# One F32 product per norm row, twelve warm-up matmuls and squares behind later casts in a decoder-trunk kernel

## The chip, the cores and the metric

The kernel runs on one NeuronCore of a Trainium2 chip. The time is device time in microseconds of one execution, from start to end; lower is better. An execution's span, from its first to its last instruction, is a little shorter than its time.

Five engines work side by side, each through its own instructions in order: PE (TensorE, matrix products), ACT (ScalarE), DVE (VectorE), POOL (GpSimd) and SP (SyncE, which here only starts transfers). They wait for each other through semaphores. PE's products go to PSUM, which ACT and DVE read; the other tiles stand in SBUF.

## The reference

One layer of a decoder trunk on 256 prompt tokens and 8 x 4 sample tokens, 2048 channels, all in F32:

```python
def trunk_layer(x, ...):
    h = rmsnorm(x, norm1_g)
    proj = einsum("btd,de->bte", h, w_in) + b_in           # 2048 -> 3072
    a, gate, z = proj[..., :1024], proj[..., 1024:2048], proj[..., 2048:]
    u = a * sigmoid(gate)
    u_ext = concatenate([hist_conv, u], axis=1)
    c = silu(layernorm(depthwise_causal_conv(u_ext, conv_w, conv_b), ln_g, ln_b))   # 31 taps
    z_ext = concatenate([hist_pool, z], axis=1)
    d = multiscale_pool(z_ext, pos0)                        # windows of 2, 4, 8, 16
    p = einsum("btgc,gce->btge", d, pool_w).reshape(bsz, T, 1024) * pool_scale
    x = x + einsum("btm,md->btd", concatenate([c, p], -1), w_out)
    h2 = rmsnorm(x, norm2_g)
    f = square(relu(einsum("btd,df->btf", h2, w_ff1)))      # 2048 -> 8192
    x = x + einsum("btf,fd->btd", f, w_ff2)
    return x, u_ext[:, -30:], z_ext[:, -15:]

def rmsnorm(x, g):
    return x * rsqrt(mean(x * x, axis=-1) + 1e-6) * g
```

A last rmsnorm follows. The layernorm over the 1024 conv channels subtracts the mean and divides by the root of the variance. So there are four places where a mean over channels becomes one inverse root per token.

## The kernel before, in words

**Layout.** Channels stand on the 128 partitions, the 288 tokens (T) along the row: `xT` has 16 slices (k) of 128 x 288. A weight matrix times activations is a run of 128 x 128 weight tiles, each with 288 columns streaming through.

**Precision.** A weight block `wr` comes by transfer from memory in F32. ACT casts it to `whi`, in a one-pass format (fp32r), and the rest `wlo` = `wr` - `whi` is formed on DVE (L279, in the first blocks L372), on POOL (L282, in two halves) or by a second transfer that accumulates (L277). Activations are split in the same way. Each weight tile then takes three matmuls: high by high, `wlo` by high, `whi` by low. `split_part` (L268) does this; which engine takes a block is set by the table `WAYS`.

**PE's order** is the program's order: `chain` (L300 to L308) ties each matmul behind the one before. `gemm` (L310) writes the products of a block, two weight slices (a pair of k) at a time; `between={key: f}` calls `f`, which puts a small product of its own into the row of matmuls at that place, and `classes` permutes the first few matmuls of a block. On the other engines a scheduler orders the instructions by a time model at build, with `later()` marking the conv taps as work for gaps.

**Start.** Nine F32 matmuls on a tile of ones (`warm`, L214) run while the first transfers are under way. `first_split` (L358) then takes the pairs of slices of `xT` as they land: it casts the weights of the first two conv heads (`whi`, L363, L370; `wlo`, L372) and scales x by the gain into `hx` (L366, L368, L375). The first `gemm` (L532) makes two conv heads, 192 matmuls; it isn't normalised yet. `squares` (L410) sums x squared over the slices: ACT squares a pair of slices (L417), DVE adds (L419 to L421), in the buffer `z_all`, into `tot`.

**First norm.** `rsqrt_sums` (L238), called by `first_sums` in the last pair of that gemm, brings the sums over the partitions onto 96 partitions x 3 columns (three small products, `pt`), and computes the inverse root there with a Sqrt on ACT and one Newton step on DVE (`st`, L249 to L256). `spread` (L259), called by `first_rows` behind the twelfth matmul of the third conv head, brings it back to a row on every partition by three products with the identity; `rb` (L529) is the row. The conv heads' results are multiplied by it afterwards (L444).

**Middle.** `SEQUENCE` (L45) gives the order of conv heads (c), pool projections (p) and pool products (P). `conv_pair` (L439) puts a head through gate, 31 taps on DVE (L460) and a reduction (L465); `pool_group` (L476) does window sums on POOL (L491 to L499) and splits the result to `dx` (L501, L502); `pool_products` (L507) multiplies it by pool_w. `sum_c` on POOL adds the conv outputs. Then the output projection runs in eight groups (L593), the pool half first; the layernorm is computed meanwhile through the table `BETWEEN` (L591): in group 5 `ln_mean` (L568), two F32 products over `sum_c` and the last conv output; in group 6 `ln_sums` (L573), the variance by `rsqrt_sums`; in group 7 `ln_rows`, `spread`. The normalised, gated result `mx` feeds the conv half of the projection.

**Second norm.** `second_rows` (L656), in the second group of the MLP: one matrix `means` on PE, Sqrt on ACT, and `inverse_root` (L231: a reciprocal and three more DVE instructions on 128 x 288).

**End.** The MLP takes four chunks of 2048 hidden channels; x is stored after the last norm, whose 96 x 3 inverse root (L726, L727) stands between the last products and the stores.

## Time and profile before

| | |
|---|---|
| median of 3 runs | 1083.33 us (1083.02 to 1084.15) |
| profiled execution: time, span | 1083.32 us, 1081.2 us |
| mean granted TensorE clock over the span | 0.997 |
| busy: PE, DVE, ACT, POOL | 99%, 59%, 44%, 16% |
| matmul records on PE | 8198 |
| read from memory | 185.16 MB, mean 175 GB/s over the span with what is written |

The busy times count instructions that overlap in the pipeline, so a busy PE says only that it never stood empty for long. What the kernel loses on PE is seen in the spacing of its matmuls: where PE is fed, one 128 x 288 matmul of the one-pass format starts every 0.13 us (572.63 us for the 4404 of the longest unbroken run). A row of the timeline gives the start, the length up to the last end, the engine, line and operation, the tiles and the count; in brackets stands the idle time ahead of it and what ended it. An F32 product leaves two records, so nine warm-up matmuls are 18.

### The profile page before, as it was taken

The page shows a single profiled execution, that of the slowest core. Times are in us where ns is not written, and L with a number is a line of the kernel's source. Part 1 is how long each engine was busy: PE and PEld are TensorE (multiplying, and loading weights), DVE is VectorE, ACT ScalarE, POOL GpSimd, SP SyncE. Part 2 cuts the span into 40 slices and gives each one's busy share as a digit, 9 for nine tenths or more (in the row PEclk, how much of TensorE's full clock was granted, in tenths as well). Part 3 has the DMA queues.
Part 4 walks back from the last instruction along what each step waited for, and adds up shares of the span by engine and source line. Part 5 has one row for each costly group of instructions (what it writes and reads, how often), then busy time and mean ns, then how long its engine had stood idle before and what let it go on. Part 6 is the DMA issues. An engine that isn't in the chain of part 4 may idle for free.

```text
span 1081.2 us, 19573 instructions
## 1 busy us (share of the span) xinstructions
PE 1069.8 (99%) x8198; PEld 1068.7 (99%) x8198; DVE 636.8 (59%) x818; ACT 477.6 (44%) x585; POOL 174.6 (16%) x180
## 2 busy tenths in 40 slices
PE   9999999999999999999999999999999999999996
PEld 9999999999999999999999999999999999999996
DVE  7899999787754544444554444555544445554553
ACT  8654445565544433334443333444433334444441
POOL 0878979512000000000000000000000000000001
PEclk9999999999999999999999999999999999999998
DMA  9896468555555555555555555555555555555522
GB/s 327 281 272 184 140 187 250 172 170 170 166 173 164 171 173 165 170 171 164 172 173 162 172 168 168 171 173 163 173 170 165 172 173 163 172 170 165 172 79 88
DMA packets 58296, 190.71 MB, mean 176 GB/s; under 512 B 6240, under 2 KB 11232, under 8 KB 58208
## 3 DMA queue, kind: packets, MB, share of 16 engines
q1 hardware_dynamic: 56336, 184.35, 54.5%
q0 software_dynamic: 1008, 3.67, 1.9%
q8 instruction: 64, 1.05, 0.4%
q10 hardware_dynamic: 864, 1.44, 0.4%
q14 instruction: 24, 0.20, 0.1%
HBM read 185.16 MB, written 4.28 MB: 175 GB/s over the span
## 4 chain that ended last, share of the span: by engine, by line
PE 76%; issue 20%; DMA 2%; DVE 1%; ACT 0%; POOL 0%; SPq 0%; POOLq 0%; DVEq 0%
PE ac L305 75%; DMA wr<-in_w 1%; PE pp L305 1%; DMA u_all<-in_hist_c 0%; DVE wlo L279 0%; POOL xT L738 0%; PE pt L305 0%; ACT whi L363 0%; DVE hx L375 0%; DVE st L255 0%; DVE wlo L372 0%; PE pmean L305 0%; ACT hx L368 0%; SPq L191 0%; POOLq L788 0%
## 5 line engine op out<-in xcount | busy, mean ns | idle before, releaser
L274 ACT CAST whi<-wr 128x1024 fp32r<-128x1024 f32 (+1 forms) x332 | 346.5, 1044 | 553.6 <-PE ac L305 540.6
L279 DVE TENSOR_TENSOR wlo<-wr,whi 128x1024 fp32r<-128x1024 f32 x288 | 353.6, 1228 | 346.0 <-ACT whi L274 346.0
L305 PE MATMUL ac<-ax,whi 128*128 128x288 f32 x2048 | 351.0, 292 | 0.0
L305 PE MATMUL ac<-fx,whi 128*128 128x288 f32 x2048 | 350.2, 292 | 0.0
L305 PEld LDWEIGHTS ac<-ax,whi 128*128 128x128 f32 x2048 | 296.0, 187 | 0.0
L305 PEld LDWEIGHTS ac<-fx,whi 128*128 128x128 f32 x2048 | 295.6, 187 | 0.0
L305 PE MATMUL ac<-ax,wlo 128*128 128x288 f32 x1024 | 217.3, 292 | 0.0
L305 PE MATMUL ac<-fx,wlo 128*128 128x288 f32 x1024 | 216.4, 292 | 0.0
L305 PEld LDWEIGHTS ac<-ax,wlo 128*128 128x128 f32 x1024 | 162.6, 187 | 0.0
L305 PEld LDWEIGHTS ac<-fx,wlo 128*128 128x128 f32 x1024 | 162.2, 187 | 0.0
L305 PE MATMUL ac<-hx,whi 128*128 128x288 f32 x768 | 131.1, 294 | 1.4 <-DVE hx L366 1.4
L738 POOL TENSOR_TENSOR xT<-xT,rf 128x288 f32<-128x288 f32 x4 | 3.1, 796 | 800.1 <-ACT rf L742 800.1
L305 PEld LDWEIGHTS ac<-hx,whi 128*128 128x128 f32 x768 | 111.8, 189 | 1.6 <-ACT hx L368 1.6
L282 POOL TENSOR_TENSOR wlo<-wr,whi 128x512 fp32r<-128x512 f32 x74 | 101.5, 1420 | 35.7 <-ACT whi L274 34.6
L460 DVE SCALAR_TENSOR_TENSOR pc<-u_all,vec,pc 128x256 f32<-128x256 f32 x232 | 99.4, 481 | 1.9 <-ACT pc L457 0.7
L305 PE MATMUL ac<-hx,wlo 128*128 128x288 f32 x384 | 80.1, 294 | 0.0
L305 PEld LDWEIGHTS ac<-hx,wlo 128*128 128x128 f32 x384 | 60.9, 189 | 0.1
L305 PE MATMUL ac<-dx,whi 128*128 128x288 f32 x256 | 46.9, 294 | 0.0
L305 PE MATMUL ac<-mx,whi 128*128 128x288 f32 x256 | 44.6, 292 | 0.0
L682 DVE SCALAR_TENSOR_TENSOR t<-ac,r 128x576 f32<-128x576 f32 x32 | 24.2, 758 | 25.3 <-PE ac L305 25.3
L305 PEld LDWEIGHTS ac<-dx,whi 128*128 128x128 f32 x256 | 38.4, 188 | 0.1
L305 PEld LDWEIGHTS ac<-mx,whi 128*128 128x128 f32 x256 | 37.4, 187 | 0.0
(133 smaller groups left out, 535.2 us busy)
## 6 DMA issues: line engine op xcount, KB each, us to landing
wr<-in_w SPq DMA_DIRECT2D x335, 512.0 KB, 3.8
wlo<-in_w POOLq DMA_DIRECT2D x7, 512.0 KB, 8.2
xT<-in_xT SPq DMA_DIRECT2D x8, 288.0 KB, 7.7
wr<-in_w SPq DMA_DIRECT2D x5, 256.0 KB, 3.7
out_u_out<-u_all SPq DMA_DIRECT2D x1, 1208.0 KB, 9.1
u_all<-in_hist_c SPq DMA_DIRECT2D x8, 136.0 KB, 5.2
out_z_out<-z_all SPq DMA_DIRECT2D x1, 668.0 KB, 9.9
z_all<-in_hist_p SPq DMA_DIRECT2D x4, 152.0 KB, 6.9
```

The lines of the kernel that those rows point to most:

```text
L274: nc.scalar.copy(hi, raw)
L279: nc.vector.tensor_tensor(lo, raw, f32(hi), op=ALU.subtract)
L282: nc.gpsimd.tensor_tensor(lo[:, j : j + 2, :], raw[:, j : j + 2, :], f32(hi[:, j : j + 2, :]), op=ALU.subtract)
L305: last = nc.tensor.matmul(*args, **kw)
L460: nc.vector.scalar_tensor_tensor(out=dst, in0=up[:, w : w + SEQ], scalar=cwv[:, w : w + 1], in1=pc, op0=ALU.mult, op1=ALU.add)
L682: nc.vector.scalar_tensor_tensor(out=t, in0=bk[:, :, :T], scalar=0.0, in1=both(rows2[0]), op0=ALU.max, op1=ALU.mult)
L738: eng.tensor_tensor(xk, xk, r[:, None, :].to_broadcast([P, n, T]), op=ALU.mult)
```

## The change

1. Warm-up: twelve `warm` matmuls for nine.
2. Norm rows: `rsqrt_sums`, `spread` and `inverse_root` go. `row_of_sums` makes one F32 product of the 128 x 128 constant `minus` (-0.5 / 2048 everywhere) with the 128 x 288 sums, which gives -0.5 times the mean on every partition at once. `row_of` takes the inverse root of the row by ACT's Abs_reciprocal_sqrt, its square by ACT, and one Newton step in two DVE instructions. The first row (`first_row`) stands whole behind the twelfth matmul of the third conv head; the product with `ones` in the last pair of the first gemm is gone. The layernorm's product stands where `ln_sums` stood; `ln_rows` is gone. The layernorm row comes out halved, so `ln_g` is doubled once on POOL.
3. The layernorm's mean: one product for two. ACT copies `sum_c` to PSUM, DVE adds the last conv output to it.
4. Second and last norm: the same inverse root, without the reciprocal. The last one has four short instructions for five.
5. Squares of x: the square of pair q is issued behind the scaling of a later slice (`scaled`): pairs 0 to 3 behind the `hx` of the fifth pair, each later one behind that of the pair after it, which leaves the last two behind the last pair.
6. The first twelve matmuls of the third conv head stand in their natural order, for the permuted one.

```diff
-        return nc.scalar.activation(few[: src.shape[0], :], src, func)
-    load_table(AF.Sqrt, ones[:, 0:1])
+        return nc.scalar.activation(few[: src.shape[0], :], src, func, scale=0.0, bias=1.0)
+    load_table(AF.Abs_reciprocal_sqrt, ones[:, 0:1])
     warm = ms("warm")
-    for j in range(9):
+    for j in range(12):
         nc.tensor.matmul(warm[:, 0, 0:P], ones, ones, start=True, stop=True)
...
+    minus = const.tile([P, P], F32, name="minus")
+    nc.gpsimd.memset(minus, -0.5 / D)
-    nc.vector.tensor_scalar(means, ones, DC / D, None, op0=ALU.mult)
+    nc.vector.tensor_scalar(means, ones, -0.5 * DC / D, None, op0=ALU.mult)
...
-    def inverse_root(mean, root, y, out):
...
-    def rsqrt_sums(parts, scale, after=None):
...
-    def spread(sums):
...
+    def row_of(psum, mean, out, scale=1.0, after=None):
+        y, y2 = psum[:, 1, :T], tmp("q")
+        nc.scalar.activation(y, mean, AF.Abs_reciprocal_sqrt, bias=eps, scale=-2.0 / scale)
+        nc.scalar.activation(y2, y, AF.Square)
         if after is not None:
+            load_table(after, y2[:, 0:1])
+        z = tmp("q")
+        nc.vector.scalar_tensor_tensor(out=z, in0=mean, scalar=-0.5 * scale * EPS, in1=y2, op0=ALU.add, op1=ALU.mult)
+        out = y if out is None else out
+        nc.vector.scalar_tensor_tensor(out=out, in0=z, scalar=1.5 * scale, in1=y, op0=ALU.add, op1=ALU.mult)
+        return out
+    def row_of_sums(total, name, *args):
+        psum = ms(name)
+        last = mm(psum[:, 0, :T], minus, total, start=True, stop=True)
+        return row_of(psum, psum[:, 0, :T], *args), last
...
-                nc.scalar.activation(hx[k][0], xT[:, k, :], AF.Copy, scale=v("norm1_g", k))
+                scaled.append(nc.scalar.activation(hx[k][0], xT[:, k, :], AF.Copy, scale=v("norm1_g", k)))
...
+    ln_g = vec[:, OFF["ln_g"] : OFF["ln_g"] + N8]
+    nc.gpsimd.tensor_scalar(ln_g, ln_g, float(D) / DC, None, op0=ALU.mult)
...
-            nc.scalar.activation(dst, xq, AF.Square)
+            with tc.issue_after(scaled[2 * min(max(q + 1, 4), 7)].ins):
+                nc.scalar.activation(dst, xq, AF.Square)
...
-    chain.append(gemm(pair0 + pair1, hx, between={15: first_sums}, classes="01" * 18 + TURN, by_part=True))
-    third = conv_products(2, between={2: first_rows}, classes="01" * 9 + TURN)
+    def first_row():
+        return row_of_sums(squares(), "norm1", rb, 1.0, AF.Sigmoid)[1]
+    chain.append(gemm(pair0 + pair1, hx, classes="01" * 18 + TURN, by_part=True))
+    third = conv_products(2, between={2: first_row}, classes="." * 12 + TURN)
...
-        norm["mean"] = ms("pmean")[:, 0, :T]
-        mm(norm["mean"], ones, sum_c[:, 0, :], start=True, stop=False)
-        return mm(norm["mean"], ones, cs[-1][:, 1, :], start=False, stop=True)
+        bk = ms("pmean")
+        norm["mean"], part = bk[:, 0, :T], bk[:, 1, :T]
+        nc.scalar.copy(part, sum_c[:, 0, :])
+        nc.vector.tensor_tensor(sum_c[:, 0, :], part, cs[-1][:, 1, :], op=ALU.add)
+        return mm(norm["mean"], ones, sum_c[:, 0, :], start=True, stop=True)
...
-        norm["sums"] = rsqrt_sums([ssc[:, 0, :]], 1.0 / DC, AF.Silu)
-        return norm["sums"][2]
-    def ln_rows():
-        norm["rows"], last = spread(norm["sums"])
+        norm["rows"], last = row_of_sums(ssc[:, 0, :], "norm2", None, float(DC) / D, AF.Silu)
         return last
-    BETWEEN = {5: {0: ln_mean}, 6: {4: ln_sums}, 7: {0: ln_rows}}
+    BETWEEN = {5: {0: ln_mean}, 6: {4: ln_sums}}
...
-        nc.scalar.activation(root, mean, AF.Sqrt, bias=eps)
-        inverse_root(mean, root, r2, r2)
+        row_of(bk, mean, r2)
...
-    nc.scalar.activation(root, sums_f, AF.Sqrt, bias=eps[:TB, :])
-    inverse_root(sums_f, root, first, s_f)
+    nc.scalar.activation(first, sums_f, AF.Abs_reciprocal_sqrt, bias=eps[:TB, :])
+    nc.vector.scalar_tensor_tensor(out=root, in0=first, scalar=-0.5, in1=first, op0=ALU.mult, op1=ALU.mult)
+    nc.vector.scalar_tensor_tensor(out=root, in0=sums_f, scalar=EPS, in1=root, op0=ALU.add, op1=ALU.mult)
+    nc.vector.scalar_tensor_tensor(out=s_f, in0=root, scalar=1.5, in1=first, op0=ALU.add, op1=ALU.mult)
```

The scheduler makes new orders of it. Three places matter here; line numbers of the changed kernel are smaller, and the numbers behind a tile's name differ between the two. On ACT in the first block, before: `whi_195` is the cast of the fourth pair's weights, `whi_204` that of the fifth's, `hx` are scaled slices, and the writes to `z_all` from `xT` are the squares.

```order
L363 CAST whi_186<-wr_100 128x1024
L368 ACTIVATE hx_197<-xT,vec 128x288 x2
L412 COPY z_all<-whi_186 128x10
L417 ACTIVATE z_all<-xT 128x576 x4
L363 CAST whi_195<-wr_103 128x1024
L368 ACTIVATE hx_206<-xT,vec 128x288 x2
L417 ACTIVATE z_all<-xT 128x576
L363 CAST whi_204<-wr_106 128x1024
```

The same place now, where the fourth pair's cast is `whi_200` and the fifth's `whi_209`:

```order
L349 CAST whi_191<-wr_100 128x1024
L354 ACTIVATE hx_202<-xT,vec 128x288 x2
L400 COPY z_all<-whi_191 128x10
L349 CAST whi_200<-wr_103 128x1024
L354 ACTIVATE hx_211<-xT,vec 128x288 x2
L406 ACTIVATE z_all<-xT 128x576 x4
L349 CAST whi_209<-wr_106 128x1024
L354 ACTIVATE hx_220<-xT,vec 128x288 x2
```

The four squares moved from ahead of the fourth pair's cast to ahead of the fifth's.

On PE, from the end of the first gemm (`wlo_238` is the last pair's rest) into the third conv head, before:

```order
L305 MATMUL pt_455<-ones,z_all 96x1 x3
L305 MATMUL ac_251<-hx_239,whi_237 128x288 x4
L305 MATMUL ac_252<-hx_239,whi_237 128x288 x2
L305 MATMUL ac_253<-hx_239,whi_237 128x288 x2
L305 MATMUL ac_502<-hx_166,whi_479 128x288 x2
L305 MATMUL ac_502<-hx_166,wlo_480 128x288 x2
L305 MATMUL ac_502<-hx_166,whi_479 128x288 x4
L305 MATMUL ac_502<-hx_166,wlo_480 128x288 x2
L305 MATMUL ac_502<-hx_166,whi_479 128x288 x2
L305 MATMUL pt_455<-ident,st_459 128x96 x3
```

And now:

```order
L291 MATMUL ac_257<-hx_244,whi_242 128x288 x4
L291 MATMUL ac_258<-hx_244,whi_242 128x288 x2
L291 MATMUL ac_259<-hx_244,whi_242 128x288 x2
L291 MATMUL ac_479<-hx_171,whi_456 128x288 x2
L291 MATMUL ac_479<-hx_171,wlo_457 128x288 x2
L291 MATMUL ac_479<-hx_171,whi_456 128x288 x4
L291 MATMUL ac_479<-hx_171,wlo_457 128x288 x2
L291 MATMUL ac_479<-hx_171,whi_456 128x288 x2
L291 MATMUL norm_509<-z_all,minus 128x288
```

Three short products twenty matmuls earlier and three at this place became one at this place; it is the first on PE to need the finished squares.

On DVE where the layernorm begins (`c_1717` is the last conv output, `ac` a group of the output projection), before:

```order
L460 SCALAR_TENSOR_TENSOR pc_1718<-u_all,vec,pc_1718 128x256 x4
L460 SCALAR_TENSOR_TENSOR c_1717<-u_all,vec,pc_1718 128x256
L600 TENSOR_TENSOR xT<-xT,ac_2535 128x576
L576 TENSOR_TENSOR c_638<-c_638,pmean_2600 128x576
L576 TENSOR_TENSOR c_722<-c_722,pmean_2600 128x576
```

And now (`c_1716`):

```order
L449 SCALAR_TENSOR_TENSOR pc_1717<-u_all,vec,pc_1717 128x256 x5
L449 SCALAR_TENSOR_TENSOR c_1716<-u_all,vec,pc_1717 128x256
L554 TENSOR_TENSOR sum_c<-pmean_2599,c_1716 128x288
L580 TENSOR_TENSOR xT<-xT,ac_2534 128x576
L560 TENSOR_TENSOR c_637<-c_637,pmean_2599 128x576
```

An addition came in between the last conv tap and the mean's product on PE.

More of the change, by code (lines that the diff above doesn't have):

```diff
@@ L224, in trunk_kernel @@
     means = const.tile([P, P], F32R, name="means")
-    nc.vector.tensor_scalar(means, ones, DC / D, None, op0=ALU.mult)
-    cst = const.tile([P, 32], F32, name="cst")
+    minus = const.tile([P, P], F32, name="minus")
+    nc.gpsimd.memset(minus, -0.5 / D)
+    nc.vector.tensor_scalar(means, ones, -0.5 * DC / D, None, op0=ALU.mult)
+    cst = const.tile([P, 64], F32, name="cst")
     eps, mean_d = cst[:, 0:1], cst[:, 1:2]
@@ L259, in spread @@
-    def spread(sums):
-        s, pr, _ = sums
-        for j in range(3):
-            last = mm(pr[:, j * TB : (j + 1) * TB], s[:, j : j + 1].to_broadcast([TB, P]), ident, start=j == 0, stop=j == 2)
-        return pr, last
+    def row_of(psum, mean, out, scale=1.0, after=None):
+        y, y2 = psum[:, 1, :T], tmp("q")
+        nc.scalar.activation(y, mean, AF.Abs_reciprocal_sqrt, bias=eps, scale=-2.0 / scale)
+        nc.scalar.activation(y2, y, AF.Square)
+        if after is not None:
+            load_table(after, y2[:, 0:1])
[4 more added lines that the diff above has]
+        return out
@@ L353, in halves @@
         return [(x2[0][:, m, :], x2[1][:, m, :]) for m in range(2)]
[L356 removed]
+    hx, firsts, scaled = [], [], []
     def first_split(k0):
@@ L559, in trunk_kernel @@
     chain.clear()
-    load_table(AF.Sqrt, f32(mixp[1][0])[:, 0:1])
+    load_table(AF.Abs_reciprocal_sqrt, f32(mixp[1][0])[:, 0:1])
     with later(2 * LATER):
```

32 lines of the change are left out of this document (2 added, 30 removed).

## The prediction

> **What bounds the kernel now.** I read the page first, then the chain of waits, the list of waits, and the timelines of the start, of the two places where a norm row is made and of the end. The page has busy times by engine (part 1) and the shares of the chain that ended last (part 4):
>
> ```profile
> PE 1069.8 (99%) x8198; PEld 1068.7 (99%) x8198; DVE 636.8 (59%) x818; ACT 477.6 (44%) x585; POOL 174.6 (16%) x180
> ...
> PE 76%; issue 20%; DMA 2%; DVE 1%; ACT 0%; POOL 0%; SPq 0%; POOLq 0%; DVEq 0%
> ```
>
> PE is the bound from its first real matmul to its last. The chain in order of time (start, length, what) shows what stands in PE's row besides the main matmuls:
>
> ```profile
> 36.51 73.77 PE ac L305 x564
> ...
> 160.21 1.56 PE pp L305 x12
> ...
> 197.74 0.97 PE pmean L305 x4
> 198.71 9.44 PE ac L305 x72
> 208.15 0.43 PE pt L305 x6
> 208.58 3.29 PE ac L305 x24
> 211.87 0.64 PE pt L305 x6
> ...
> 283.23 572.63 PE ac L305 x4404
> ```
>
> 572.63 / 4404 = 0.130 us is PE's pace when fed, and 36.51 to 110.28 holds it too (0.131). So a gain must take work off PE's row, fill a hole in it, or shorten the two ends. PE's timeline of the start shows the hole:
>
> ```profile
> 1.04 4.21 PE L214 MATMUL warm<-ones 128*128 128x128 f32 x18 [1.04 <-DVE cst L229]
> 6.61 1.30 PE L305 MATMUL ac<-hx,whi 128*128 128x288 f32 x4 [1.36 <-DVE hx L366]
> 7.71 1.16 PE L305 MATMUL ac<-hx,wlo 128*128 128x288 f32 x4
> 8.67 1.69 PE L305 MATMUL ac<-hx,whi 128*128 128x288 f32 x8
> 10.19 0.70 PE L305 MATMUL ac<-hx,wlo 128*128 128x288 f32 x4
> ...
> 18.68 1.21 PE L305 MATMUL ac<-hx,wlo 128*128 128x288 f32 x8
> ...
> 32.22 0.59 PE L305 MATMUL pt<-ones,z_all 128*96 128x1 f32 x6
> 32.67 1.57 PE L305 MATMUL ac<-hx,whi 128*128 128x288 f32 x10
> ...
> 35.13 0.43 PE L305 MATMUL ac<-hx,whi 128*128 128x288 f32 x2
> 35.61 0.91 PE L305 MATMUL pt<-ident,st 96*128 96x96 f32 x6
> 36.30 0.51 PE L305 MATMUL ac<-hx,whi 128*128 128x288 f32 x2
> ```
>
> From 7.71 to 8.67 four matmuls take 0.96 us, 0.24 each: half pace, though nothing is waited for. From 10.19 on they run at 0.13. The granted-clock column shows 1.00 here, so I go by the spacing. 184 matmuls (192 less the last 8) stand between 6.61 and 32.22: 25.61 us for 23.92 at full pace, so 1.69 us are lost.
>
> **The change part by part.**
>
> *Warm-up.* The first warm-up starts at 1.04, the last of 18 records ends by 5.25 (1.04 + 4.21), 0.22 to 0.23 us a record. Six more end at 6.5 to 6.65; the first real matmul waits until 6.61 for DVE's `hx` anyway, so they cost 0, at most 0.04. What they do is close the gap of 1.36 us ahead of 6.61. The rows show half pace before and after that gap, full pace about 3 us behind it: a rise that needs unbroken work of some 3 us is what they fit, and twelve warm-ups give 5.4 us of it before 6.61. I take full pace from 6.61; the ends are that (1.69 gained if nothing else is late) and no change (0).
>
> [...]
>
> *What then is late at the start.* ACT's and DVE's timeline:
>
> ```profile
> 7.48 0.62 ACT L370 CAST whi<-wr 128x512 fp32r<-128x512 f32 x1 [1.04 <-DMA wr<-in_w]
> ...
> 8.22 0.96 ACT L368 ACTIVATE hx<-xT,vec 128x288 fp32r<-128x288 f32 x2
> ...
> 9.53 0.62 ACT L363 CAST whi<-wr 128x512 fp32r<-128x512 f32 x1 [0.34 <-DMA wr<-in_w]
> ...
> 13.59 2.41 ACT L417 ACTIVATE z_all<-xT 128x576 f32<-128x576 f32 x4
> 14.88 2.49 DVE L419 TENSOR_TENSOR z_all<-z_all 128x576 f32<-128x576 f32 x3 [0.17 <-ACT z_all L417]
> 15.90 1.04 ACT L363 CAST whi<-wr 128x1024 fp32r<-128x1024 f32 x1
> 17.29 1.22 DVE L372 TENSOR_TENSOR wlo<-wr,whi 128x1024 fp32r<-128x1024 f32 x1
> ...
> 25.84 1.04 ACT L363 CAST whi<-wr 128x1024 fp32r<-128x1024 f32 x1
> ```
>
> Weights land 2.05 us apart (7.48, 9.53), faster than PE's 24 x 0.13 = 3.12 us for a pair. At full pace PE takes nine matmuls of the first half block until 7.78, then waits for the second half's cast (ends 8.10): 0.35 lost. It ends the pair at 10.08 and waits for the cast that ends at 10.15: 0.07. From then the pairs begin at 13.27, 16.39, 19.51. Without the moved squares the fourth pair's rest, done at 18.51 (17.29 + 1.22) for a matmul at 18.68 today, would be 1.1 us late at 17.43. With them behind, its block lands at about 13.6 (9.53 and twice 2.05), is cast by 14.65, and the rest is done by 15.9. The four squares then stand ahead of the fifth cast: 14.65, two scalings 0.96, squares 2.41, cast 1.04 give 19.1 for 19.51, and the rest, which on DVE comes behind three additions that end 0.6 or more behind the squares and takes 1.22, is done at 20.3 to 20.5 for 20.55. No wait, but little room. The sixth to eighth pair each take ACT 2.6 (0.96, one square 0.60, 1.04), the last 0.6 more: last cast by 27.5 to 28.2 for PE at 28.87. Loss 0.42 in place of 1.69: **1.27** gained (0 to 1.69).
>
> *First norm row.* Before, the sums hold PE from 32.22 to 32.67, 0.45, and the spreading from 35.39 (two matmuls behind 35.13) to 36.30, 0.91, with a short wait for `st` in it. Now one F32 product; the nearest row is `pmean`, two such products in 0.97, so 0.49. Gain **0.87** (0.8 to 1.1, the rows behind each product being a little wide). PE reaches the product behind the last pair (28.87 + 3.12) and twelve matmuls, at 33.6. The sum of squares before and the row `rb`:
>
> ```profile
> 29.27 1.43 DVE L421 TENSOR_TENSOR z_all<-z_all 128x288 f32<-128x288 f32 x1
> ...
> 36.56 0.40 ACT L529 COPY rb<-pt 128x288 f32<-128x288 f32 x1
> ```
>
> The sum was done at 30.70. Now the last additions come behind a cast that ends up to 1.3 later than the 26.88 that the last pair's cast (25.84 and 1.04) had, so I expect it by 31.8 to 32.0: 1.6 us of cover. Abs_reciprocal_sqrt stands in no row. Its nearest is Sqrt on the same shape, also out of PSUM, 0.48; the ends are the copy's 0.40 and a pair's square, 0.60 for twice the columns.
>
> ```profile
> 283.86 0.48 ACT L666 ACTIVATE mean<-mean,cst 128x288 f32<-128x288 f32 x1
> 284.37 1.96 DVE L233 RECIPROCAL r<-mean 128x288 f32<-128x288 f32 x1 [0.56 <-ACT mean L666]
> ```
>
> Two steps of 0.5 on ACT and two on DVE behind 34.1 give the row at about 36.2, 0.8 sooner than 36.96. PE doesn't wait for it; DVE does.
>
> *Layernorm.* Mean: one product for two, **0.49** gained (0.97 / 2). Variance: 208.15 to 211.87 is 3.72 for 24 matmuls (3.12), so 0.60, and 0.64 for the spreading; 1.24 less 0.49 is **0.75**. ACT's copy of `sum_c` has its operand long before; the addition on DVE (under 0.5) stands in the way of PE:
>
> ```profile
> 194.30 0.48 DVE L460 SCALAR_TENSOR_TENSOR c<-u_all,vec,pc 128x256 f32<-128x256 f32 x1
> ...
> 197.58 0.65 PE L305 MATMUL pmean<-sum_c,ones 128*128 128x288 f32 x2
> ```
>
> Room today 197.58 - 194.78 = 2.8 us. PE will come 1.27 + 0.87 = 2.14 earlier and the addition takes 0.5: 0.2 left, if DVE is not sooner.
>
> *Second norm.* The reciprocal of 1.96 us goes from DVE and a square joins ACT; PE is fed by other work there. 0: the long run from 283.23 shows no hole that today's later row made; it would cost only if the row came so late that the third group found no free bank.
>
> *Small things.* POOL's two new instructions (filling `minus`, doubling `ln_g`) stand ahead of its first subtraction, which waits for the third head's weights; the natural order of that head's first twelve matmuls is the one they already had; no transfer is added or dropped, and on SP's queue only the store of the pool state slips ahead of one weight block. 0 each, in the spread of the lateness below.
>
> *End.* One DVE instruction of 0.27 goes from the path (1070.03 to 1070.30 in these rows), **0.27** (0 to 0.3):
>
> ```profile
> 1070.03 0.17 DVE L233 RECIPROCAL cst<-cst 96x3 f32<-96x3 f32 x1 [1.53 <-ACT cst L726]
> 1070.30 0.16 DVE L234 SCALAR_TENSOR_TENSOR cst<-ends,cst 96x3 f32<-96x3 f32 x1
> ```
>
> *What is late next.* Between 40 and 190 us DVE and POOL are nearly full, and their work doesn't all move with PE. The tightest place is the third pool product:
>
> ```profile
> 158.64 0.75 DVE L502 TENSOR_TENSOR dx<-d,dx 128x576 fp32r<-128x576 f32 x1
> ```
>
> Its `dx` is done at 159.39 for a product at 160.21: 0.82 room. PE comes 2.14 earlier, the DVE chain at least the 0.8 of the row; if no more, PE waits 0.5, if nothing moves 1.3. For less speaks that DVE's waits for PE in this stretch (in the list: 1.7 for L444, 0.8 for L482) shrink when PE is early. I take **-0.4** (0 to -1.3), with the even case at the mean in it.
>
> ```profile
> DVE ac L444 <- PE ac L305: 1.7, 3, 0.7
> ...
> DVE tz L482 <- PE ac L305: 0.8, 1, 0.8
> ```
>
> Sum: 1.27 + 0.87 + 0.49 + 0.75 + 0.27 = 3.65, less 0.4 is 3.25 us. The profiled execution took 1083.32 us with a span of 1081.2; the 2.1 us around it I leave. It stands at the median of 1083.33, so 1083.3 - 3.2 = **1080.1**.
>
> **The rivals.** A change that can be told from none here is over 0.2%, 2.2 us: below 1081.2 is faster, above 1085.5 slower.
>
> *No earlier full pace.* The pace may rise at a fixed time or need more than the gap closed; or the runs of before may often have been quick already, the profiled one not. Then 1.27 falls away, and so does most of the lateness downstream, since PE is 0.87 ahead only: 3.65 - 1.27 - 0.2 = 2.2, **1081.1**, at the bound of what can be told. For it speaks that one trace shows one rise; against, that half pace lasts beyond 6.61 just where the gap lies.
>
> *The feeding engines don't follow.* 1.3 at the pool product, and 0.5 at the mean or the fifth pair: 3.65 - 1.8 = 1.85, **1081.5**. For it: DVE's fullness; against: the waits for PE.
>
> *Slower: the product on the squares stalls PE.* PE's row is fixed, so if the sum of squares came late, all behind it stands. It costs nothing until 33.6, then each us costs one; to be slower by 2.2 us the sum must come 3.2 + 2.2 us after 33.6, at 39.0, some 7 us later than worked out. ACT's and DVE's work up to there is only reordered, so little speaks for it. **Over 1085.5.**
>
> **How the numbers follow.** Forecast case 0.68 (its own range from 1079.2, the sum with 1.69 and no lateness, to 1081.1), no earlier pace 0.15, feeding engines 0.12, slower 0.05. The first holds the likeliest time. The range runs from a little below its lower end, 1078.9, to 1081.8, past both middle rivals. Faster: 0.68 and half of 0.15, 0.76; same: the other half and the 0.12, 0.19; slower 0.05.
>
> **What would show it.** Right: matmuls at 0.13 from 6.6 us on and the first gemm over at about 32; the fourth and fifth pairs without a hole; two `norm` records of about 0.24 apart; no hole at the third pool product; reciprocals gone. Wrong: spacings of 0.24 after 6.61, a wait of PE on `z_all`, `dx` or `sum_c`, or the addition into `sum_c` waiting on ACT's copy.

## The result: 0.5% slower, and the profile after

The changed kernel took 1089.21 us, the median of 5 runs (1087.76 to 1089.87); the kernel before took 1083.02 us in 5 runs beside it. The ratio is 1.0053, with a 95% interval of 1.0042 to 1.0064: slower by about 6 us, where 3.2 us less was forecast. The profiled execution of the changed kernel is its quickest, 1087.76 us with a span of 1085.9 us; what the clocks of the others show is told at the end.

The page still has PE busy for 99% of the span, but the chain that ended last is another one (engines with busy time and instructions, then shares of the chain by engine):

```profile
PE 1071.1 (99%) x8182; PEld 1068.3 (98%) x8182; DVE 637.8 (59%) x810; ACT 478.6 (44%) x588; POOL 176.5 (16%) x182
...
PE 68%; issue 21%; DVE 5%; POOL 3%; DMA 2%; ACT 1%; POOLq 0%; SPq 0%
```

PE's share of it fell from 76% to 68%, and DVE, POOL and DMA, 3% together before, have 10%. The busy times hardly moved (PE 1069.8 us before, POOL 174.6): no engine got much more work. PE's list of waits (line, what it waited for, us in total, times, longest) names the places:

```profile
PE ac L291 <- DMA wlo<-in_w: 2.5, 1, 2.5
PE warm L214 <- DVE cst L231: 1.0, 1, 1.0
PE ac L291 <- DVE dx L503: 1.0, 2, 0.9
PE pp L291 <- DVE dx L491: 0.9, 1, 0.9
PE ac L291 <- ACT whi L356: 0.3, 1, 0.3
```

In before the list had one wait behind the warm-up, 1.4 us for `hx`. That one is gone. New are 2.5 us for `wlo` from an accumulating transfer (the residual block made by way "D") and three waits for `dx`, 1.9 us together. The chain in order of time shows the same stretch (start, length, what):

```profile
41.26 8.35 DMA wlo<-in_w
49.65 6.36 PE ac L291 x46
56.01 9.17 DMA wlo<-in_w
65.23 22.40 PE ac L291 x166
88.85 2.54 POOL wlo L268 x2
...
132.42 2.51 DVE dx L491
...
182.12 21.34 PE ac L291 x162
...
288.19 572.63 PE ac L291 x4404
```

Two transfers (issued at 41.26 and 56.01) and then, from 88.85 to 182.12, first POOL and then DVE carry the chain. From 288.19 on the long run is what it was, 572.63 us for 4404 products.

To see where time goes I number PE's main products (`ac` and `pp` rows, 8112 in every kernel) in order of time and take the start of the n-th against the start of the n-th before. Negative is ahead of before; each column is one profiled execution, worked out from the rows of PE:

| before, us | changed | e4 | e5 | e10 | e11 | e9 |
|---|---|---|---|---|---|---|
| 13.4 | -0.72 | -0.97 | -1.62 | -1.53 | -1.55 | -0.74 |
| 29.1 | -0.43 | -0.98 | -1.00 | -1.53 | -1.56 | -0.74 |
| 41.2 | -1.38 | -1.25 | -0.93 | -0.69 | -0.61 | -1.84 |
| 62.0 | -0.75 | -1.26 | -0.93 | -0.69 | -0.25 | -0.07 |
| 67.2 | +2.14 | -1.26 | -0.93 | -0.69 | -0.12 | +0.06 |
| 150.7 | +2.37 | -0.99 | -1.15 | -0.49 | +0.13 | +0.29 |
| 161.1 | +3.93 | +0.57 | -1.15 | +1.28 | +0.13 | +1.85 |
| 182.0 | +5.72 | +2.49 | -1.15 | +2.19 | +1.01 | +3.77 |
| 220.8 | +4.70 | +1.87 | -2.15 | +1.18 | +0.40 | +3.15 |
| 286.2 | +4.96 | +2.14 | -1.89 | +1.45 | +0.67 | +3.42 |

The changed kernel is 1.38 us ahead at 41 us. It loses 0.6 us from there to 62 us (a spacing of 0.37 at 49.3, at the block that the first transfer fills, and a slower pace behind it), 2.9 us between 62 and 67, and 3.35 us between 150 and 182 at the pool products; the layer norm gives 1.0 back. The other columns are experiments.

### The profile page after: what moved, and what is told of

Its sections match the earlier page's. It is cut to its first block, busy times and chain, and to the rows that moved or that the text cites. A ratio compares the mean times of both kernels' runs of the same rounds, so it can differ in the third digit from the quotient of the medians.

```text
span 1085.9 us, 19541 instructions
## 1 busy us (share of the span) xinstructions
PE 1071.1 (99%) x8182; PEld 1068.3 (98%) x8182; DVE 637.8 (59%) x810; ACT 478.6 (44%) x588; POOL 176.5 (16%) x182
## 3 DMA queue, kind: packets, MB, share of 16 engines
q8 instruction: 64, 1.05, 0.4%
## 4 chain that ended last, share of the span: by engine, by line
PE 68%; issue 21%; DVE 5%; POOL 3%; DMA 2%; ACT 1%; POOLq 0%; SPq 0%
PE ac L291 67%; DVE pc L449 3%; DMA wlo<-in_w 2%; POOL wlo L268 1%; POOL s L480 1%; DVE wlo L265 1%; DMA wr<-in_w 1%; DVE d L485 0%; DVE dx L491 0%; DVE dx L503 0%; POOL xT L719 0%; DVE c L454 0%; POOL prd L452 0%; ACT whi L260 0%; DVE u_all L437 0%
## 5 line engine op out<-in xcount | busy, mean ns | idle before, releaser
L291 PE MATMUL ac<-hx,whi 128*128 128x288 f32 x768 | 131.3, 294 | 0.5 <-ACT whi L356 0.3
```

The lines of the kernel that those rows point to most:

```text
L291: last = nc.tensor.matmul(*args, **kw)
```

## The experiments

Two theories stood at the start. *Row*: the first norm row's new place makes row, sigmoids and residual blocks late. *Start*: PE, 1.3 us ahead, runs into blocks and projections that come no sooner. After the first four runs a third took the lead, *order*: the edits let the scheduler put the instructions of DVE, ACT and POOL in another order up to 190 us, and that order is worse.

The medians, with before on the same chip and the ratio to it:

| run | us | before | ratio, 95% interval |
|---|---|---|---|
| e1_start | 1086.14 | 1083.74 | 1.0026 (1.0016 to 1.0035) |
| e2_late | 1081.72 | 1083.74 | 0.9984 (0.9975 to 0.9993) |
| e3_no_late_transfer | 1091.21 | 1083.74 | 1.0069 (1.0055 to 1.0083) |
| e4_row_early | 1085.19 | 1083.74 | 1.0011 (1.0002 to 1.0020) |
| e5_late_and_warm | 1081.06 | 1083.62 | 0.9978 (0.9968 to 0.9987) |
| e6_squares_back_row_early | 1082.43 | 1083.62 | 0.9989 (0.9981 to 0.9998) |
| e7_squares_back | 1090.17 | 1083.62 | 1.0053 (1.0040 to 1.0065) |
| e8_start_split_product | 1084.69 | 1083.62 | 1.0009 (1.0000 to 1.0018) |
| e9_negative_copy_pinned | 1086.24 | 1083.43 | 1.0024 (1.0015 to 1.0033) |
| e10_late_and_start | 1084.75 | 1083.43 | 1.0009 (1.0000 to 1.0018) |
| e11_late_start_pinned | 1082.27 | 1083.43 | 0.9989 (0.9980 to 0.9998) |
| e12_changed_split_product | 1088.74 | 1083.43 | 1.0049 (1.0035 to 1.0062) |

The medians of before in the three groups, and in the comparison above, lie up to 0.7 us apart; a difference between two rows with another before is good to about that much.

**e1_start**, twelve warm-ups and the moved squares alone, in the kernel before:

```diff
-    for j in range(9):
+    for j in range(12):
...
-            nc.scalar.activation(dst, xq, AF.Square)
+            with tc.issue_after(scaled[2 * min(max(q + 1, 4), 7)].ins):
+                nc.scalar.activation(dst, xq, AF.Square)
```

> The kernel before with only the start changed: twelve warm-up products, and the squares of x behind later conversions; the first norm row stands where it was, with its old three products, and so do the other norms. Theory 'row' (the loss comes from the first norm row's new place, which puts the sigmoids of the gates and the residual's blocks later): the start keeps its 1.27 us, so 1081.8 us, and the second block of the fifth head (wlo after a transfer) is waited for under 1.5 us. Theory 'start' (TensorE ahead by 1.3 us runs into blocks and projections that come no sooner): the gain is eaten and waits come on top, 1083 to 1086 us, with over 1 us at that block and holes at the pool products between 160 and 182 us. Theory 'pace' (products every 133 ns for 130 ns up to 92 us follow from the early start): 133 ns here as well, worth about 1.5 us.

Measured 2.4 us slower than before, where 1.27 us less was the prediction's term. PE is never held at the fifth head's block; the holes are at the pool products, 2.1 us in all (0.95 and 0.84 at 159 to 161, 0.67 at 171.8, less 0.13 each). PE's lead of 1.0 us at 41 us is still there at 100 us, so *pace* is wrong too. *Row* is wrong for these holes. *Start* has their place right, but not the wait at the fifth head nor its reason: an engine that came no sooner would bring PE back to before, not behind it. Something on DVE came later than before. The timeline (start, length, engine) shows `dx`, DVE's subtraction behind the pool sums, and `prd`, POOL's product for the new samples of a conv head, in before and then in e1:

```profile
129.25 2.21 POOL L463 TENSOR_TENSOR prd<-u_all,vec 128x992 f32<-128x992 f32 x1
...
131.08 1.00 DVE L502 TENSOR_TENSOR dx<-d,dx 128x576 fp32r<-128x576 f32 x1
```

```profile
129.31 2.20 POOL L464 TENSOR_TENSOR prd<-u_all,vec 128x992 f32<-128x992 f32 x1 [1.25 <-DVE u_all L449]
...
129.54 2.59 DVE L503 TENSOR_TENSOR dx<-d,dx 128x576 fp32r<-128x576 f32 x1
```

In before the subtraction starts 0.38 us ahead of the product's end and takes 1.00 us. In e1 it starts 0.23 us behind the product's start and lasts until 132.13, 0.62 us behind the product's end, as if it had done its work only then. In e1's order DVE has one tap of the conv between `u_all`, which lets `prd` go, and `dx`; in before's it has five.

In before, too, the subtraction ends 0.62 us behind the product's end. I read both as a wait for the product, which the prediction did not weigh; e8 tries it with a shorter product.

**e2_late**, the later norms alone (mean, variance, second and last norm as in the change; nine warm-ups, squares and first row as before):

> The kernel before with only the later norms changed (LN mean and LN variance by one F32 product each, second norm and last norm by the new root); nine warm-up products, squares and first norm row as before. All theories: what the trace of after shows of these parts stays, 0.49 + 0.75 + 0.27 = 1.5 us faster, 1081.6 us. If it is 1083 us or more, the later norms hold a loss that the trace of after did not show.

Measured 2.0 us faster. This part is as forecast within its interval, and hides no loss.

**e3_no_late_transfer**, the changed kernel with the late block on another engine:

```diff
-"c4": "GDGD"
+"c4": "GVGD"
```

> The changed kernel, with the second residual block of the fifth head subtracted by VectorE (way V) instead of by GpSimd's accumulating transfer (way D). Theory 'transfer has no slack': the 2.68 us wait at 62.42 us goes; if nothing later hangs on the same time, 1089.2 - 2.7 = 1086.5 us. Theory 'VectorE and GpSimd are late by themselves' (the projections' pool sums end last between 100 and 182 us): TensorE reaches the pool products 2.7 us sooner and waits there 2.7 us longer, so 1089 us, or more, since VectorE gets a subtraction of about 0.5 us more.

Measured 1091.21 us, 2 us more than the changed kernel. Neither number came, and the run doesn't tell the theories apart: the subtraction that was to take 0.5 us took 9.12. DVE's row of the timeline, then POOL's:

```profile
49.57 9.12 DVE L265 TENSOR_TENSOR wlo<-wr,whi 128x1024 fp32r<-128x1024 f32 x1
```

```profile
45.20 7.79 POOL L268 TENSOR_TENSOR wlo<-wr,whi 128x512 fp32r<-128x512 f32 x6
52.69 2.43 POOL L452 TENSOR_TENSOR prd<-u_all,vec 128x992 f32<-128x992 f32 x1
54.83 2.77 POOL L268 TENSOR_TENSOR wlo<-wr,whi 128x512 fp32r<-128x512 f32 x2
57.32 1.12 POOL L263 DMA_DIRECT2D wlo<-in_w  x1
```

The same shape takes 1.21 us at 138.38 in the changed kernel. Here it ends at 58.69, 1.09 us behind the end of POOL's chain of subtractions (57.60): by these rows DVE got in only when POOL came to a transfer. What follows on DVE came some 6 us later than in the changed kernel (it releases the next head's `prd`, at 69.06 for 62.98), and the next transfer, issued at 71.18, kept PE waiting 5.7 us at 73 us.

**e4_row_early**, the changed kernel with the one product of the row back among the first gemm's products:

```diff
-    chain.append(gemm(pair0 + pair1, hx, classes="01" * 18 + TURN, by_part=True))
+    chain.append(gemm(pair0 + pair1, hx, between={15: first_row}, classes="01" * 18 + TURN, by_part=True))
-    third = conv_products(2, between={2: first_row}, classes="." * 12 + TURN)
+    third = conv_products(2, classes="." * 12 + TURN)
```

> The changed kernel, with the one product of the first norm row put back among the first projection's products (at part 15) instead of inside the third conv block. Theory 'row': table load and row come some 3 us sooner, the sigmoid of the first gate no longer waits for them, and the waits at the fifth head's block (2.68 us) and at the pool products (2.7 us) shrink to under half: 1085 to 1087 us. Theory 'start': the row's place matters little, 1088.5 to 1089.5 us. The row's product would also wait for the sums of squares itself at that place: a hole of up to 2 us at about 26 us.

Measured 1085.19 us, 4.0 us less than the changed kernel. The wait for the transfer is gone: *row* holds for that. As expected, the row's product waits at its new place for the squares, 0.5 us. The holes at the pool products stay (1.24, 1.16 and 0.46 us in PE's spacings, against 1.23, 1.16 and 0.45 of the changed kernel), and the subtraction takes 2.60 us at 128.99: here *row* fails, and e1 had it too. So there are two losses.

**e5_late_and_warm** puts twelve warm-ups into e2_late, and leaves DVE's, ACT's and POOL's order up to the layer norm as it was before:

> The kernel before with the later norms as in e2_late, and twelve warm-up products. The squares of x and the first norm row stand as before, so that up to 190 us VectorE, ScalarE and GpSimd get their instructions in exactly the order of before. Theory 'order' (the loss of e1_start comes from the order that the moved squares bring about on VectorE, ScalarE and GpSimd, not from TensorE being ahead): the order of before stands, so the pace from 6.6 us on is kept in part; the fourth pair's rest is then 1 us late, so 0.3 to 1.0 us less than e2_late, 1080.8 to 1081.5 us, and the dx subtraction at about 131 us takes 1.0 us. Theory 'TensorE's lead' (whatever is gained at the start is lost at the pool products): 1081.7 us or more, as e2_late, with holes at the pool products as long as the lead.

Measured 1081.06 us, 2.6 less than before, and no hole at the pool products, as *order* has it. This is the fastest kernel of the study. The lead of the start stands in the table: 1.62 us at 13 us, 1.00 at 29 us after a spacing of 0.40 and one of 0.24 at the fourth pair, and it is kept through 182 us. A lead of PE by itself, 1 us here, does no harm.

**e6_squares_back_row_early**: the changed kernel with squares and row both back in place (e4's edit, and the squares' `issue_after` taken out):

> The changed kernel with two things put back: the squares of x are not held behind later conversions, and the one product of the first norm row stands among the first projection's products (part 15). VectorE and GpSimd then have the order of before from the first residual to the layer norm. Theory 'order': the other gains stand (0.87 of the row, 1.5 of the later norms, some of the start), 1079.5 to 1080.8 us, no dx subtraction of 2.6 us, no wait over 0.6 us at the fifth head or at the pool products. Theory 'TensorE's lead': TensorE is 1.5 to 2 us ahead of before at 60 us and waits about as long between 140 and 182 us: 1081.7 to 1083 us.

Measured 1082.43 us. No long subtraction (0.98 us at 131.50) and no hole above 0.35 us between 60 and 230 us, as *order* has it; but 1.6 us over the upper end of its forecast. Its trace shows two losses. The larger is at the start: at 29 us PE is 0.48 us behind before, where e5 is 1.00 ahead. The second half's cast came late (a spacing of 0.64 us at 7.7), and with the squares in their old place the fourth pair's cast and rest are late (0.48 at 16.8, 0.54 at 18.3). Then PE has a spacing of 0.26 us at 50.2, at the block that the first transfer fills, and from there to 90 us a product takes 133 ns instead of 130 (see the last section).

**e7_squares_back**: the changed kernel with the squares alone back:

> The changed kernel with the squares of x alone put back: the norm row stays inside the third conv block. VectorE's and GpSimd's order is then again another than that of before. Theory 'order' with the row's place as a cause of its own: table load and row late, sigmoid behind casts, the transfer for the fifth head issued late: 1085 to 1089 us, with a wait of 2 us or more at 62 us. Theory 'the squares do it all': as e6, 1079.5 to 1081 us.

Measured 1090.17 us (1086.8 to 1091.35), over the upper end of the first theory. The row's place is a cause of its own: the edits of e6 and e7 differ in nothing else, and it costs 7.7 us there, 5.4 between the quickest executions of the two, and 4.0 us between e4 and the changed kernel. PE waits 3.3 us for the fifth head's transfer. e7 also loses 3.4 us between 150 and 182 us, with the squares back in place. There is no long `dx` subtraction at that point (0.76 us at 134.21), but the residual block at 138.31 takes 3.05 us beside `prd`: in another order, other instructions of DVE and POOL meet.

**e8_start_split_product**: e1_start, with the `prd` that runs beside the long subtraction cut in four; the order is e1's.

```diff
-            nc.gpsimd.tensor_tensor(prd[:, :, :, 0:CW], windows(us, CW), ...)
+            halves_p = 4 if i == 6 else 1
+            for j in range(halves_p):
+                n = NB // halves_p
+                nc.gpsimd.tensor_tensor(prd[:, j * n : (j + 1) * n, :, 0:CW], windows(us[:, j * n : (j + 1) * n], CW), ...)
```

> e1_start with one edit: GpSimd's product for the new samples of the seventh head (prd, 2.2 us, the one that runs while VectorE's dx subtraction at 129.5 us takes 2.59 us) is issued as four products of a quarter each; the order of all else is that of e1_start. Theory 'the subtraction waits for the GpSimd instruction that is running': it gets in behind a quarter, takes 0.8 to 1.4 us, and what follows on VectorE comes 1.2 to 1.8 us sooner; the holes at the pool products between 145 and 175 us shrink by as much: 1084.5 to 1085 us. Theory 'GpSimd lets VectorE in only when it pauses': the subtraction takes 2.6 us or more again, 1086.1 us. Theory 'the long subtraction does not matter': shorter, but the time stays at 1086.1 us.

Measured 1084.69 us, 1.45 less than e1. The two rows of the timeline:

```profile
130.68 3.14 POOL L467 TENSOR_TENSOR prd<-u_all,vec 128x248 f32<-128x248 f32 x4 [1.24 <-DVE u_all L449]
...
130.91 1.08 DVE L506 TENSOR_TENSOR dx<-d,dx 128x576 fp32r<-128x576 f32 x1
```

The subtraction ends at 131.99, 1.83 us ahead of the last quarter's end (133.82): it got in behind a quarter. PE's holes of 0.95 and 0.84 at 159 to 161 us are gone. This is the first theory, with its number. In the two traces PE is 1.3 us behind e1's at 140 us, for reasons ahead of the edit, and 0.8 us ahead of it at 182: 2.1 us, somewhat more than forecast.

**e9_negative_copy_pinned**: the changed kernel, with ACT's negative copy for the first accumulating transfer held behind the sigmoids of heads 0 and 1 (for this the third head's weights are made ready behind `conv_pair(1)`, so that the sigmoids exist; `gated` is a list of them):

```diff
-            nc.scalar.activation(lo, f32(hi), AF.Copy, scale=-1.0)
+            with tc.issue_after(gated[1].ins) if len(gated) == 2 else nullcontext():
+                nc.scalar.activation(lo, f32(hi), AF.Copy, scale=-1.0)
```

> The changed kernel with one thing held in order: on ScalarE, the negative copy for the first accumulating transfer comes behind the sigmoids of heads 0 and 1, as before the change. What follows from it in the order: GpSimd issues the first transfer behind the first two prd products instead of ahead of them, and the one for the fifth head (issued at 56.01 us in the changed kernel, landed at 65.18) ahead of the prd product that took 53.87 to 56.0. Theory 'the transfer has no slack': it is issued 2 to 2.5 us sooner, the 2.68 us wait at 62.42 us goes to under 0.7; the clock no longer drops behind it: 1085.5 to 1087 us. Theory 'VectorE is late by itself' (row and sigmoids late, a locked subtraction at 132 us): the wait at 62 us goes too, but the holes at the pool products grow from 2.7 to 5 us: 1088.5 to 1089.5 us.

Measured 1086.24 us, 3.0 less than the changed kernel (1.5 between the two profiled executions). The number is the first theory's; its detail is only partly so. The drop of the clock that it puts behind the wait is not in the changed kernel's profile (a granted clock of 1.00 from 58 to 88 us); e7's has one, told at the end. POOL's two transfers with the products ahead of them in e9, then the second one in the changed kernel and in before:

```profile
40.23 4.33 POOL L454 TENSOR_TENSOR prd<-u_all,vec 128x992 f32<-128x992 f32 x2 [0.98 <-DVE u_all L439]
44.52 1.02 POOL L264 DMA_DIRECT2D wlo<-in_w  x1
...
52.80 2.42 POOL L454 TENSOR_TENSOR prd<-u_all,vec 128x992 f32<-128x992 f32 x1
54.94 1.11 POOL L264 DMA_DIRECT2D wlo<-in_w  x1
```

```profile
53.87 2.40 POOL L452 TENSOR_TENSOR prd<-u_all,vec 128x992 f32<-128x992 f32 x1
56.01 1.11 POOL L263 DMA_DIRECT2D wlo<-in_w  x1
```

```profile
53.04 2.36 POOL L463 TENSOR_TENSOR prd<-u_all,vec 128x992 f32<-128x992 f32 x1
55.19 1.05 POOL L277 DMA_DIRECT2D wlo<-in_w  x1
```

The second transfer still stands behind the product and is issued 1.07 us sooner, not 2 to 2.5. It also lands sooner, in 7.59 us for 9.17. But the first one, issued 3.26 us later, now holds PE for 1.39 us at 48.8 (it landed in 5.8 us, at 50.29), and that is room for the second. In before this transfer landed at 50.60 for a product at 50.80, so PE's lead of 1.84 us at 41 us could not pass this place: at 62 us it is 0.07. One wait of 1.4 us took the place of one of 2.7 and one of 0.24. The holes at the pool products are those of the changed kernel, 3.5 us in the table.

**e10_late_and_start** is e5 with the moved squares; **e11_late_start_pinned** is e10 with e9's hold.

> e5_late_and_warm with the squares of x held behind later conversions, as in the change; the first norm row stands as before. The order on VectorE, ScalarE and GpSimd is that of e1_start. Theory 'order': 2.0 us less than e1_start and 3 us more than e5, 1084.1 us. If the squares' move were harmless by itself: 1080.6 us, since the hole of 0.4 us at the fourth pair goes.

> e10_late_and_start with the negative copy held behind the sigmoids of heads 0 and 1, as in e9. VectorE and GpSimd then have the order of before past the dx subtraction at about 130 us. Theory 'order' (the one exchange on ScalarE brings the loss, through the order that follows from it): the dx subtraction takes 1.0 us again, no hole over 0.5 us at the pool products, 1080.6 to 1081.3 us, 3 us less than e10. Theory 'the squares' move costs by something else': 1083.5 to 1084.5 us, as e10.

Measured 1084.75 and 1082.27 us. e10 is what *order* said within 0.7 us; e11 gains in the way *order* said, but is 1.0 us over the upper end of its forecast. So the squares' move costs 3.7 us over e5, and one exchange on ACT (negative copy or sigmoids first) takes 2.5 of them off again. Their subtractions, e10 and e11:

```profile
130.13 2.60 DVE L519 TENSOR_TENSOR dx<-d,dx 128x576 fp32r<-128x576 f32 x1
```

```profile
131.21 1.13 DVE L521 TENSOR_TENSOR dx<-d,dx 128x576 fp32r<-128x576 f32 x1
```

The squares do at the start what the prediction said: -1.53 us held from 13 to 29 us, where e5 falls back to -1.00. But the sum of squares is then late for the old row's first product (a spacing of 0.83 us at 30.5 in e11), and the lead is down to -0.6 at 41 us. e11 is 1.2 us over e5: a hole of 0.73 us at 171, and 133 ns a product from 50 us on. Its order is not quite that of before either: some conv taps on DVE and some pool sums on POOL stand in other places.

**e12_changed_split_product**: e8's edit in the changed kernel.

> The changed kernel with the edit of e8 alone: the seventh head's prd product on GpSimd as four quarters, all else in the same order. Theory 'the locked subtraction sets the pool products': the subtraction at 132.3 us takes 0.8 to 1.4 us instead of 2.59, the holes between 162 and 182 us shrink from 2.7 us to 1.2 or so: 1087.7 us. Theory 'the holes there come from the late sigmoids alone': under 0.4 us less, 1088.9 us.

Measured 1088.74 us, 0.5 us less than the changed kernel (0.9 if each is taken against the before beside it): nearer to the second theory, and the trace has its holes. DVE's rows:

```profile
131.02 1.08 DVE L494 TENSOR_TENSOR dx<-d,dx 128x576 fp32r<-128x576 f32 x1
...
135.54 1.98 DVE L265 TENSOR_TENSOR wlo<-wr,whi 128x1024 fp32r<-128x1024 f32 x1
...
139.40 2.03 DVE L265 TENSOR_TENSOR wlo<-wr,whi 128x1024 fp32r<-128x1024 f32 x1
```

The subtraction is short, as in e8, and yet PE's holes are unchanged (spacings of 1.23, 1.18 and 0.46 us). The two residual blocks behind it now take 1.98 and 2.03 us, where they took 1.21 and 1.28 in the changed kernel: the 1.5 us that were won. In the changed kernel the long subtraction (2.59 us) is a place where DVE's time goes, but shortening it alone gives nothing: the time goes a little later, in these two blocks.

## Why the prediction was wrong

*The start, 1.27.* Half right. PE runs at full pace from 6.65 us, as said, and the wait for the second half's cast is there:

```profile
6.65 0.77 PE L291 MATMUL ac<-hx,whi 128*128 128x288 f32 x4
...
7.78 0.30 PE L291 MATMUL ac<-hx,whi 128*128 128x288 f32 x1
8.42 1.19 PE L291 MATMUL ac<-hx,whi 128*128 128x288 f32 x7 [0.34 <-ACT whi L356]
```

The fourth and fifth pairs have no hole. The earlier full pace holds in every trace: with nine warm-ups (before and e2) the spacings of 0.24 last until 9.4 us, with twelve no such stretch is left behind 6.7 us in any of twelve executions. The lead is 0.72 us at 13 us, and 1.5 to 1.6 in three other executions (e5, e10, e11) where that half's cast began at 6.1 to 6.4 instead of 7.75: the term lies between 0.7 and 1.6 by the execution. What came on top is the pace of 133 ns, which took 0.3 us by 29 us. The rival of no earlier pace is wrong. That of feeding engines that don't follow is wrong for a lead by itself, since e5 keeps its own; in the changed kernel they do worse than not follow.

*First norm row, 0.87.* Right for PE: from -0.43 to -1.38, 0.95, with no wait on the squares. Wrong for the row itself, which was to be 0.8 us sooner than 36.96 and was ready at 37.38: its product came at 34.54 for 33.6, and DVE's first step on it at 36.45, behind a residual block. ACT's rows show what came behind it, in the changed kernel and then in before:

```profile
35.23 0.48 ACT L236 ACTIVATE norm<-norm,cst 128x288 f32<-128x288 f32 x1 [3.10 <-PE norm L291]
35.73 0.41 ACT L237 ACTIVATE q<-norm 128x288 f32<-128x288 f32 x1
36.04 1.04 ACT L260 CAST whi<-wr 128x1024 fp32r<-128x1024 f32 x1
37.10 1.28 ACT L209 ACT_TABLE_LOAD   x1
...
38.50 1.03 ACT L260 CAST whi<-wr 128x1024 fp32r<-128x1024 f32 x1
39.57 1.06 ACT L262 ACTIVATE wlo<-whi 128x1024 fp32r<-128x1024 f32 x1
40.53 0.87 ACT L435 ACTIVATE tg<-ac,vec 128x288 f32<-128x288 f32 x2
```

```profile
33.27 1.28 ACT L209 ACT_TABLE_LOAD   x1
...
39.18 0.88 ACT L446 ACTIVATE tg<-ac,vec 128x288 f32<-128x288 f32 x2
```

The kernel loads the sigmoid's table behind the row's last step on ACT. Before, that load stood at 33.27, 3 us ahead of the row; now it stands behind the row's product, and a cast and the negative copy (`wlo`<-`whi`) come ahead of the sigmoid `tg`, at 40.53 for 39.18 before. `u_all`, `prd` and, on POOL's queue behind `prd`, the fifth head's transfer (56.01 for 55.19) follow. The load itself (1.28 us) is the smaller part: in e9 it also stands behind the row's product, at 36.63, but the copy comes behind `tg`, and `tg` begins at 38.98. In before and in e6 the copy comes behind `tg`; the squares' hold without the row's new place (e1, e4, e10) and that place without the hold (e7) each bring it ahead. I priced the row's arithmetic and not the order that ACT would get.

*What is late next, -0.4 (0 to -1.3).* This is the step that failed. It names the right place, the third pool product, and there alone the loss is 1.6 us; with the others it is 3.35 us, and the fifth head's transfer, 2.9 us with the pace, is not in it at all. Two things were left out. The seven accumulating transfers were not looked at for room. In before the first landed at 50.60 for a product at 50.80, and the second, issued at 55.19, at 62.23 for one at 63.28: 0.2 and 1.05 us of room, where the sum lets PE come 2.14 earlier. In the changed kernel the second held PE for 2.7 us: PE's lead of 0.75, the later issue of 0.82 and a longer way to landing, 2.1 (9.17 us for 7.04), together used up the room and 2.65 more. The longer way is the largest of the three. The three kernels with this wait (the changed one, e7, e12) have 8.5 to 9.6 us there, and all others in which a transfer makes this block have 6.6 to 7.6. Why it took longer no run shows. And the order of work was taken as fixed: "their work doesn't all move with PE" assumes that it only shifts. It was reordered, by the squares' hold (3.7 us, e10 against e5) and by the row's place (e7 against e6), and the place where an instruction of DVE is drawn out beside POOL's work moved with it (`dx` with 1.00 us in before and 2.59 in the changed kernel, a residual block with 3.05 in e7). The slower rival, given 0.05, named the time and not the mechanism: the sum of squares was done at 32.08, 2.5 us ahead of its product, and PE did not wait for it. What it says in its own disfavour, "only reordered, so little speaks for it", shows the slip: a new order was taken as free.

*Layer norm, 0.49 and 0.75.* From +5.72 to +5.24 and to +4.70: 0.48 and 0.54. The products are as forecast (two records each in 0.65 us, the first at 203.30 and 213.22), the room at the mean was enough, and the variance is 0.2 short. Another 0.26 goes by 247 us, at 224.7, where PE has two spacings of 0.24 at `mx`.

*End, 0.27.* Right: +4.96 at 286 us, +4.7 in the span.

What stays open: how the 7.7 us of e7 against e6 split between the row's lateness and the other order that it brings (no run has the row late in the order of before); and which pairs of DVE and POOL instructions make the changed kernel's holes at the pool products, since e12 freed one pair and kept the holes.

## What to carry to other kernels

Where a scheduler sets the order, one hold can exchange two instructions on one engine and the rest of the stage follows; compare the orders of every engine for the whole stage, and try the edit alone before it is priced as a shift. Where DVE and POOL are both nearly full (busy for 143.6 and 131.3 of the 150 us from 40 to 190 us in before), look at which subtraction of DVE meets which POOL work: here it ended 0.6 to 1.1 us behind that work (2.59 us for 1.00 in e1, 9.12 for 1.21 in e3), and the place moves with the order. For every transfer that PE waits on, write issue, landing and first use side by side: one with little room (1.05 us in before, at the fifth head) can turn a delay of the stages ahead into a wait of PE (2.7 us in the changed kernel).

## What the runs showed of the hardware

*The pace has two values.* From 100 to 136 us and in the long run behind 288 us a 288-column product takes 130.0 ns in before and in the changed kernel; behind some short waits of PE it takes about 133 on average for 10 to 40 us. The changed kernel at 50 to 60 us, then before (stretch, PE's busy time and records, clock, DMA share, GB/s):

```profile
50.00:60.00 10.00, 10.00 (x77) 1.00 0.83 235
```

```profile
50.00:60.00 10.00, 10.00 (x79) 1.00 0.82 241
```

The granted clock is 1.00 in both. In before the slow pace starts at a spacing of 0.22 us at 78.9, in e6 at one of 0.26 at 50.2, in e4 at one of 0.36 at 77.5; by 95 us all are at 130.0 again. It cost e6 0.6 us. What holds it there is not known.

*The two longest waits cost twice.* In e7 the products at 62.3 and 65.9 are 3.57 us apart, and 1.4 us behind that the clock halves (the columns are those above):

```profile
66.00:67.00 1.00, 1.00 (x8) 1.00 0.96 209
67.00:68.00 1.00, 1.00 (x7) 0.61 1.04 369
68.00:69.00 1.00, 1.00 (x6) 0.50 1.09 406
69.00:70.00 1.00, 1.00 (x6) 0.50 1.00 254
70.00:71.00 1.00, 1.00 (x7) 0.69 1.08 242
```

Products come every 0.24 us from 67.3 to 70.5, and by these rows the clock is at half for 3.4 us. In e3 PE stood for 5.7 us from 73.4; there the clock is at half for 6.8 us, from 77.7, still in the wait, to 84.5:

```profile
80.00:84.00 4.00, 4.00 (x18) 0.50 0.90 292
```

In the profiled execution of the changed kernel the spacing of 2.81 us has no such stretch, at a mean granted clock of 0.998; its other executions, 1.1 to 2.1 us longer, have 0.994 to 0.997. e7 splits likewise: 1086.8 and 1087.0 us at 0.998, 1090.2 to 1091.4 at 0.994 to 0.996. That most executions of the changed kernel lose this time as well is an inference from the clocks, and a weak one: executions of before have 0.996 to 0.998. The half clock lasts 3.4 us in e7 and twice that in e3. How long PE must wait for it no run here shows: the wait was 3.3 us in e7 by the list of waits, and 2.5, without a drop, in the changed kernel.

*A subtraction of DVE can last through several instructions of POOL.* The 9.12 us of e3 span six of POOL's subtractions and products that follow each other without a gap, while in e8 `dx`, with 1.08 us, was done ahead of the last quarters of `prd`. What decides it no run here shows.
